# A bidirectional RWKV-7 recurrence: inverses of two steps in one batch, score matrices per head as row tiles, matmul groups kept together, and low-rank weights padded to full height

## The chip, the cores and the metric

The kernel runs on one core of one Trainium2 chip. The metric is the time of one execution on the device, in microseconds (us).

## The reference, cut to what matters

One encoder layer is applied to 1280 tokens (one request of 1024, one of 256; width 1024): a SwiGLU half step, a combined projection, two mixers (RWKV-7 in both directions, and attention), two branch projections with gates, an output projection, and a second SwiGLU half step. What is changed lies in the RWKV mixer, with 8 heads of 64 channels and two directions. Its core is a scan over the tokens for each head and direction:

```python
def _rwkv7_step(S, inp):
    r, w, k, v, kk, b = inp
    sa = jnp.einsum('dbhij,dbhj->dbhi', S, -kk)
    S = S * w[..., None, :] + sa[..., :, None] * b[..., None, :] + v[..., :, None] * k[..., None, :]
    y = jnp.einsum('dbhij,dbhj->dbhi', S, r)
    return S, y
```

The decay `w` and the rate `a` come from low-rank products: `w0 + tanh(wd) @ w_up` and `a0 + ad @ a_up`, with 64 low-rank columns for each direction.

## The kernel before

The layer runs in stages: the first SwiGLU, the projections of attention, attention interleaved with dense columns, the RWKV columns with their preparation (`columns`, `prep`), the recurrence (`run`), the branch projections, the output projection, and the second SwiGLU. A framework (Tile) gives out buffers and semaphores and orders each engine's instructions by readiness and priority; a call traced under `high_priority` goes ahead of others that are ready.

**Preparation.** `prep` works on 20 pieces: 4 pairs of heads (q) times 5 chunks of 256 tokens. For each piece and each direction d it makes two products, for the decay and for the rate: a matmul L576 with the high part of the weights (128 rows, in which the low-rank activations' high and low part lie one above the other) and a matmul L577 with the low part of the weights, which has only the 64 rows of its direction. ScalarE takes the sum through a tanh (L578). The pieces are interleaved with the projections (L165), which have no part in the change.

**Recurrence.** The scan is done in chunks of 64 tokens. A step is one chunk forward and one chunk backward for a pair of heads; there are 4 pairs of heads with 20 steps each, 80 steps in all. A step has three parts.

- `front`: the scores G of both directions, one 128x128 by 128x256 matmul for each direction (L676; the moving operand AR holds both heads side by side, with zeros in the other head's rows), masked on VectorE into `gs` (L683); two transposes of BK (L681), copied to `BKt` by ScalarE (L685); the blocks `Bm` and `Bl` cut out of `gs` by GpSimd (L692, L696).
- `inv`: the inverse of a triangular matrix for each of two heads, by doubling in fp16: a start on GpSimd and VectorE (L709, L711), five rounds of matmuls (L715), a masked eviction on VectorE (L717), matmuls (L720, L721) and an eviction on ScalarE (L723), then a correction (L726 to L733). Up to four inverses run at a time, each in its own PSUM bank.
- `chain`: what hangs on the state S. Matmuls L752 (64x64 tiles) and L756 (128x64 tiles) sum to z, ScalarE copies it (L759), L763 (64x64) makes u, ScalarE copies that (L764, L765), L771 (128x64) makes the update of S, and VectorE and GpSimd make the new S (L785, L786). L778 and L780 (128x64) make the output yp, which L792 or L794 puts into YT.

An f32 matmul is two instructions on TensorE, an fp16 one is one. `run` steps through these generators in a fixed order of ticks: in each, up to four inverses advance by one part, two places take a part of chain or front, and two take a part of `finish`, which normalizes a done pair of heads. `front` runs ahead of `chain` by up to `NB` = 7 steps.

PSUM has 8 banks: 4 for inverses, 1 for G, 1 for z, u and the update of S, 1 shared by the transposes, yp and `finish`, and 1 (`psD`) that belongs already to the next stage, so that the first products of the branch projection (L1156) can run while the recurrence still does.

Of the kernel before, what the change touches and what calls it, by code (L numbers as in the profile page):

```python
# [21 lines left out]
TT = 10  # L22
# [320 lines left out]
class Bufs:  # L343
# [5 lines left out]
    def tile(self, shape, dt, name, tag=None):  # L349
# [7 lines left out]
PQ = (4, 3)  # L357
PBT = "pb"
# [6 lines left out]
       "TT": 7, "tt": 9, "y1": 6, "zs": 2, "Sn": 3, "SP": 2}  # L365
RPB = {"i": 4, "g": 1, "z": 1, "s": 1}
# [5 lines left out]
BD = 1  # L372
# [8 lines left out]
class Rwkv:  # L381

    NB, PK, LAG, NAR, AHEAD, NI = 7, 1, 2, 8, 1, 4
# [41 lines left out]
    def prep_weights(self, q, W):  # L425
# [17 lines left out]
    def loop_consts(self, ep, cp):  # L443
# [10 lines left out]
        for i in range(self.NB):  # L454
            bm = cp.tile([128, 2, 128], F16, name=f"Bm{i}")
            bl = cp.tile([128, 2, 128], F16, name=f"Bl{i}")
# [103 lines left out]
    def prep(self, q, got, ci, W, ps):  # L560
# [10 lines left out]
        for d in range(2):  # L571
            ds_ = slice(64 * d, 64 * d + 64)
# [11 lines left out]
        o = W.tile([128, n], F32, name="go", tag="go")  # L584
# [80 lines left out]
    def front(self, pp, sd, cf, cb, W, ps, TG, res):  # L665
# [7 lines left out]
        g = ps.tile([128, 4, 128], F32, name="g", tag=TG["g"])  # L673
        for d in range(2):
            AR, BK = sd[d]
            nc.tensor.matmul(g[:, 2 * d:2 * d + 2], lhsT=BK[:, cs[d] % 4], rhs=AR[:, cs[d] % 4], start=True, stop=True)  # L676
            if d == 0:
                yield
        tr = ps.tile([128, 2, 128], F32, name="tr", tag=TG["x"])
        for d in range(2):  # L680
            nc.tensor.transpose(tr[:, d], sd[d][1][:, cs[d] % 4], self.k.ident)  # L681
        gs = W.tile([128, 4, 128], F32, name="gs", tag="gs")
        nc.vector.tensor_tensor(out=gs, in0=g, in1=self.gm, op=ALU.mult)  # L683
        BKt = W.tile([128, 2, 128], F32, name="BKt", tag="BKt")
        nc.scalar.copy(BKt, tr)  # L685
        Bm, Bl = self.Bm[self.step_no % self.NB], self.Bl[self.step_no % self.NB]
# [10 lines left out]
        TT_ = W.tile([128, 2, 128], F32, name="TT", tag="TT")  # L697
        res.update(gs=gs, BKt=BKt, UV=UV, TT=TT_, Bm=Bm, Bl=Bl)
        yield

    def inv(self, ind, W, ps, TG):

        nc = self.nc
        Bm, Bl = ind["Bm"], ind["Bl"]
        p = ps.tile([128, 4, 128], F32, name="inv", tag=TG["i"])
        m, dbl = p[:, 0:2], p.rearrange("p (h a) t -> p h a t", h=2)
        mask = lambda l: self.lv[:, l:l + 1].to_broadcast([128, 2, 128])
        tt = W.tile([128, 2, 2, 128], F16, name="tt", tag="tt")
# [4 lines left out]
        for l in range(1, 6):  # L713
            for h in range(2):
                nc.tensor.matmul(m[:, h], lhsT=Bm[:, h], rhs=tt[:, h, 0], start=True, stop=True)  # L715
            y1 = W.tile([128, 2, 128], F16, name="y1", tag="y1")
            nc.vector.tensor_tensor(out=y1, in0=m, in1=mask(l), op=ALU.mult)  # L717
            yield
            for h in range(2):
                nc.tensor.matmul(dbl[:, h, 0], lhsT=tt[:, h, 1], rhs=y1[:, h], start=True, stop=True)  # L720
                nc.tensor.matmul(dbl[:, h, 1], lhsT=y1[:, h], rhs=tt[:, h, 1], start=True, stop=True)  # L721
            tt = W.tile([128, 2, 2, 128], F16, name="tt", tag="tt")
            nc.scalar.copy(tt, dbl)  # L723
            yield
        for h in range(2):
            nc.tensor.matmul(m[:, h], lhsT=Bm[:, h], rhs=tt[:, h, 0], start=True, stop=False)  # L726
            nc.tensor.matmul(m[:, h], lhsT=Bl[:, h], rhs=tt[:, h, 0], start=False, stop=True)
        ws = W.tile([128, 2, 128], F16, name="ws", tag="y1")
        nc.vector.tensor_tensor(out=ws, in0=m, in1=tt[:, :, 0], op=ALU.subtract)
        yield  # L730
        for h in range(2):
            nc.tensor.matmul(m[:, h], lhsT=ws[:, h], rhs=tt[:, h, 1], start=True, stop=True)
        nc.vector.scalar_tensor_tensor(out=ind["TT"], in0=tt[:, :, 1], scalar=2.0, in1=m, op0=ALU.mult, op1=ALU.add)  # L733
        yield

    def chain(self, pp, sd, st, cf, cb, ind, W, ps, TG, first, early):
# [11 lines left out]
        for h in range(2):  # L748
            hs = slice(64 * h, 64 * h + 64)
            for d in range(2):  # L750
                vr = rows(1 - d)
# [560 lines left out]
```

## Time and profile before

| | |
|---|---|
| time, median of 3 runs | 3557.76 us (3557.45 to 3557.83) |
| the profiled execution: its time, its span | 3558.98 us, 3557.2 us |
| TensorE, VectorE, ScalarE, GpSimd busy | 97%, 48%, 36%, 11% of the span |
| granted TensorE clock, mean over the span | 0.988 of 2.4 GHz |

The span is the time from the first to the last instruction; the profiled execution's time is 1.8 us longer. A busy TensorE is not one at its peak: matmuls are pipelined, and the record of one is longer than the distance to the next. What a matmul takes from the others is the distance from its start to the next start, and that is how the rows of the timeline below are to be read.

### The profile page before, as it was taken

To read this page: it belongs to the slowest core of one execution; us is meant where nothing else is said; L and a number is where in the kernel's file an instruction comes from. 1 tells how busy PE (TensorE), PEld (TensorE's weight loads), DVE (VectorE), ACT (ScalarE), POOL (GpSimd) and SP (SyncE) were. 2 spreads that over 40 slices of the span, in tenths; PEclk is the share of its full clock that TensorE was granted. 3 is DMA by queue.
4 is the path that set the end of the run, shared out by engine and by line. 5 is a ranking of instruction groups with operands and counts; after the bars stand their busy time and mean duration, and the time that the engine had idled before them with its cause. 6 is when DMAs were issued, how large, how long until landed. Compare 5 with 4: busy or idle time off the path is not lost. (4 is left out here: it accounts for less than half of the span.)

```text
span 3557.2 us, 56074 instructions
## 1 busy us (share of the span) xinstructions
PE 3467.9 (97%) x22608; PEld 2907.8 (82%) x22608; DVE 1720.8 (48%) x3300; ACT 1291.6 (36%) x2524; POOL 376.7 (11%) x706
## 2 busy tenths in 40 slices
PE   8999999999899999999989999998999999999997
PEld 7888888888788888887768888888878888888886
DVE  3233333333726776648777667647332333333335
ACT  4211111111523666746556666623432111111112
POOL 0000000000301000003144444410000000000002
PEclk9999999999999999999999999999999999999999
DMA  3111111111324121224352212147221111111103
GB/s 127 42 36 36 36 48 36 42 36 35 131 83 135 59 73 45 84 77 154 130 184 85 70 54 76 41 146 236 102 83 36 42 36 36 36 45 39 36 30 119
DMA packets 155108, 264.93 MB, mean 74 GB/s; under 512 B 16864, under 2 KB 98016, under 8 KB 154720
## 3 DMA queue, kind: packets, MB, share of 16 engines
q1 hardware_dynamic: 154848, 261.34, 22.9%
q8 instruction: 178, 2.92, 0.3%
q14 instruction: 82, 0.67, 0.1%
HBM read 183.94 MB, written 74.06 MB: 73 GB/s over the span
## 5 line engine op out<-in xcount | busy, mean ns | idle before, releaser
L165 PE MATMUL pp<-hT,whi 128*128 128x512 f32 (+1 forms) x6000 | 1643.1, 360 | 7.8 <-ACT qk L950 4.9
L165 PEld LDWEIGHTS pp<-hT,whi 128*128 128x128 f32 x6000 | 1068.0, 190 | 175.6 <-ACT qk L950 5.7
L165 PE MATMUL pp<-hT,wlo 128*128 128x512 f32 (+1 forms) x3000 | 1074.4, 358 | 0.0
L165 PEld LDWEIGHTS pp<-hT,wlo 128*128 128x128 f32 x3000 | 569.3, 190 | 79.8
L141 DVE TENSOR_TENSOR wlo<-wraw,whi 128x1024 fp32r<-128x1024 f32 x125 | 154.1, 1233 | 566.7 <-ACT whi L140 566.6
L211 DVE TENSOR_TENSOR acc<-acc,pd 128x512 f32<-128x512 f32 x400 | 271.3, 685 | 203.4 <-PE pd L206 203.2
L206 PE MATMUL pd<-dh,ah 128*128 128x512 f32 x880 | 346.4, 394 | 13.8 <-DVE acc L211 13.8
L206 PE MATMUL pd<-dh,al 128*128 128x512 f32 x880 | 345.6, 393 | 0.0
L206 PE MATMUL pd<-dl,ah 128*128 128x512 f32 x880 | 345.4, 392 | 0.0
L293 POOL TENSOR_TENSOR yg<-acc,gb 128x1024 f32<-128x1024 f32 x19 | 48.2, 2544 | 2075.1 <-DMA xb<-x_d 1128.6
L723 ACT CAST tt<-inv 128x512 f16<-128x512 f32 x400 | 226.6, 588 | 90.7 <-PE inv L721 66.4
L187 DVE TENSOR_TENSOR sg<-sg,pp 128x512 f32<-128x512 f32 x132 | 79.0, 598 | 347.8 <-PE pp L165 347.8
L140 ACT CAST dh<-draw 128x1024 fp32r<-128x1024 f32 x44 | 46.0, 1046 | 528.8 <-DMA draw<-wd 528.8
L140 ACT CAST ah<-sg 128x512 fp32r<-128x512 f32 x132 | 72.2, 547 | 439.5 <-DVE sg L187 439.5
L206 PEld LDWEIGHTS pd<-dh,ah 128*128 128x128 f32 x880 | 166.7, 189 | 52.0 <-DVE acc L211 18.1
L717 DVE TENSOR_TENSOR y<-inv,lv 128x256 f16<-128x256 f32 x400 | 161.6, 418 | 83.6 <-PE inv L715 61.4
L140 ACT CAST whi<-wraw 128x1024 fp32r<-128x1024 f32 x125 | 131.1, 1049 | 194.1 <-PE pp L165 191.7
L206 PEld LDWEIGHTS pd<-dh,al 128*128 128x128 f32 x880 | 166.7, 189 | 35.3
L206 PEld LDWEIGHTS pd<-dl,ah 128*128 128x128 f32 x880 | 166.6, 189 | 33.8
L178 ACT ACTIVATE sg<-pp 128x512 f32<-128x512 f32 x132 | 69.1, 524 | 327.1 <-PE pp L165 325.8
L1156 PE MATMUL pbr<-yT,whi 128*128 128x256 f32 x640 | 124.1, 291 | 19.2 <-ACT yT L140 8.9
L720 PE MATMUL inv<-y,tt 128*128 128x128 f16 x800 | 130.7, 221 | 0.0
(228 smaller groups left out, 4868.3 us busy)
## 6 DMA issues: line engine op xcount, KB each, us to landing
wraw<-wgu SPq DMA_DIRECT2D x88, 512.0 KB, 3.5
draw<-wd SPq DMA_DIRECT2D x44, 512.0 KB, 3.8
gate_d<-go SPq DMA_DIRECT2D x16, 640.0 KB, 3.2
ar_d<-ar SPq DMA_DIRECT2D x40, 256.0 KB, 2.1
bk_d<-bk SPq DMA_DIRECT2D x40, 256.0 KB, 2.1
AR<-ar_d SPq DMA_DIRECT2D x80, 128.0 KB, 2.9
BK<-bk_d SPq DMA_DIRECT2D x40, 256.0 KB, 2.9
g<-gate_d SPq DMA_DIRECT2D x80, 128.0 KB, 3.3
```

The source lines that it names most:

```text
L140: self.nc.scalar.copy(dst_h, src)
L141: self.nc.vector.tensor_tensor(out=dst_l, in0=src, in1=dst_h.bitcast(F32), op=ALU.subtract)
L165: nc.tensor.matmul(p[:, :n], lhsT=a[:, ks], rhs=h[:, b, k], start=i == 0, stop=i == 23)
L178: nc.scalar.activation(out=sg[:, c0:c0 + n], in_=p[:, :n], func=AF.Silu)
L187: nc.vector.tensor_tensor(out=sg[:, s], in0=sg[:, s], in1=p[:, :n], op=ALU.mult)
L206: nc.tensor.matmul(p, lhsT=a[:, ts], rhs=b[:, hs], start=i == 0, stop=i == m - 1)
L211: nc.vector.tensor_tensor(out=acc[:, t, hs], in0=acc[:, t, hs], in1=p, op=ALU.add)
L293: (nc.vector if late else nc.gpsimd).tensor_tensor(out=yg, in0=y, in1=gbc, op=ALU.mult)
L717: nc.vector.tensor_tensor(out=y1, in0=m, in1=mask(l), op=ALU.mult)
L720: nc.tensor.matmul(dbl[:, h, 0], lhsT=tt[:, h, 1], rhs=y1[:, h], start=True, stop=True)
L723: nc.scalar.copy(tt, dbl)
L1156: nc.tensor.matmul(p, lhsT=a[:, ks], rhs=ys[ci][:, b, kk], start=i == 0, stop=i == 11)
```

## The change

It does five things.

- `inv` takes the four matrices of two steps at once: every tile and every instruction of it is twice as wide, the PSUM tile has two banks, and two of them are open at a time, not four. Two steps share one `Bm`, `Bl` and `TT` tile, and an inverse starts when both steps' fronts are there.
- G is made per head: four matmuls with 64 rows (heads in rows 0 to 63 and 64 to 127), 128 columns of weights and a moving operand of 128 columns, so 8 instructions of 64x128 tiles in place of 4 of 128x128. The heads go to two banks, and the transposes go into the first of these.
- `together` chains the matmuls of a group on TensorE, each behind the one before, and gives them priority. G, z, u, and the update of S with yp are such groups. In z the part with S now goes first, and the part with UV after it. The update takes the backward direction first.
- `chain` gives up control three times in a step and no more five, `front` still twice.
- In `prep` the low part of the weights has 128 rows, the other direction's set to zero by GpSimd, so L577 becomes a 128x128 matmul over all rows. The tile `go` takes its buffer from the three of `w1`.

PSUM is then 4 banks for inverses, 2 for G and the transposes, 1 for z, u and the update, 1 for yp and `finish`; `psD` is gone, and the branch projection takes all its banks when the recurrence is done.

```diff
-RWB = {... "TT": 7, "tt": 9, "y1": 6, ...}
-RPB = {"i": 4, "g": 1, "z": 1, "s": 1}
+CP = 300
+RWB = {... "TT": 4, "tt": 5, "y1": 4, ...}
+RPB = {"i": 2, "g": 1, "z": 1, "s": 1}
...
-    NB, PK, LAG, NAR, AHEAD, NI = 7, 1, 2, 8, 1, 4
+    NB, PK, LAG, NAR, AHEAD, NI = 7, 3, 2, 8, 1, 2
...
-        lo = W.tile([128, 2, 128], F32R, name="llo")
+        lo = W.tile([128, 2, 2, 128], F32R, name="llo")
         for d in range(2):
-            rs = slice(64 * d, 64 * d + 64)
-            nc.vector.tensor_tensor(out=lo[rs], in0=raw[rs, d], in1=hi.bitcast(F32)[rs, d], op=ALU.subtract)
+            rs, ot = slice(64 * d, 64 * d + 64), slice(64 - 64 * d, 128 - 64 * d)
+            nc.vector.tensor_tensor(out=lo[rs, d], in0=raw[rs, d], in1=hi.bitcast(F32)[rs, d], op=ALU.subtract)
+            nc.gpsimd.memset(lo.bitcast(F32)[ot, d], 0.0)
...
-                nc.tensor.matmul(p[:, j], lhsT=lo[ds_, j], rhs=src[ds_, d, cs], start=False, stop=True)
+                nc.tensor.matmul(p[:, j], lhsT=lo[:, d, j], rhs=src[:, d, cs], start=False, stop=True)
...
-        o = W.tile([128, n], F32, name="go", tag="go")
+        o = W.tile([128, n], F32, name="go", tag="w1")
...
-        g = ps.tile([128, 4, 128], F32, name="g", tag=TG["g"])
-        for d in range(2):
-            AR, BK = sd[d]
-            nc.tensor.matmul(g[:, 2 * d:2 * d + 2], lhsT=BK[:, cs[d] % 4], rhs=AR[:, cs[d] % 4], start=True, stop=True)
-            if d == 0:
-                yield
-        tr = ps.tile([128, 2, 128], F32, name="tr", tag=TG["x"])
+        g = ps.tile([128, 2, 4, 128], F32, name="g", tag=TG["g"])
+        with self.together() as go:
+            for d in range(2):
+                AR, BK = sd[d]
+                for h in range(2):
+                    hs = slice(64 * h, 64 * h + 64)
+                    go(g[:, h, d], lhsT=BK[hs, cs[d] % 4], rhs=AR[hs, cs[d] % 4, h], start=True, stop=True)
+        tr = g[:, 0, 2:4]
...
+    @contextlib.contextmanager
+    def together(self):
+        tc, last = self.k.tc, []
+        def go(out, **kw):
+            with tc.issue_after(last[-1].ins) if last else contextlib.nullcontext():
+                last.append(self.nc.tensor.matmul(out, **kw))
+        with tc.high_priority(offset=CP):
+            yield go
...
-        for h in range(2):
-            hs = slice(64 * h, 64 * h + 64)
-            for d in range(2):
-                vr = rows(1 - d)
-                nc.tensor.matmul(z[rows(d), h], lhsT=gs[vr, 2 * d + h, 0:64], rhs=UV[vr, d, hs], start=h == 0, stop=first and h == 1)
-        if not first:
+        with self.together() as go:
+            if not first:
+                for h in range(2):
+                    for d in range(2):
+                        go(z[rows(d), h], lhsT=sd[d][0][:, cs[d] % 4, h, 0], rhs=S[:, d], start=h == 0, stop=False)
             for h in range(2):
+                hs = slice(64 * h, 64 * h + 64)
                 for d in range(2):
-                    nc.tensor.matmul(z[rows(d), h], lhsT=sd[d][0][:, cs[d] % 4, h, 0], rhs=S[:, d], start=False, stop=h == 1)
+                    vr = rows(1 - d)
+                    go(z[rows(d), h], lhsT=gs[vr, 2 * d + h, 0:64], rhs=UV[vr, d, hs], start=first and h == 0, stop=h == 1)
...
-        psD = early.enter_context(tc.tile_pool(name="psD", bufs=1, space=PSUM))
...
-                    for _ in branch(1, yb_d, I["wbb"], WD, lambda dt, ci: psD if dt < BD or ci == 0 else ps, emit_mb, WD):
+                    for _ in branch(1, yb_d, I["wbb"], WD, lambda dt, ci: ps, emit_mb, WD):
```

## Rows read from the trace of the kernel before

**Rows 1.** Busy time and instructions of each engine, granted clock and DMA, two stretches.

```profile
core 0: us, PE busy (x) PEld busy (x) DVE busy (x) ACT busy (x) POOL busy (x), PEclk, DMA share, GB/s
1860.00:2310.00 450.00, 446.15 (x6390) 362.54 (x6390) 314.91 (x837) 300.46 (x726) 206.83 (x430) 1.00 0.23 68
...
2044.00:2068.16 24.16, 24.11 (x362) 19.70 (x361) 16.53 (x44) 15.35 (x36) 11.18 (x24) 1.00 0.20 56
```

**Rows 2.** Waits of TensorE, 1860 to 2310 us: total, times, longest.

```profile
PE inv L715 <- DVE tt L711: 3.2, 3, 1.1
```

**Rows 3.** Timeline of TensorE: start, duration, instruction.

```profile
2045.49 0.22 PE L721 MATMUL inv<-tt,y 128*128 128x128 f16 x1
2045.64 0.45 PE L763 MATMUL zu<-zs,TT 64*64 64x64 f32 x8
2046.02 0.28 PE L715 MATMUL inv<-tt,Bm 128*128 128x128 f16 x2
...
2048.43 0.33 PE L756 MATMUL zu<-Sn,AR 128*64 128x64 f32 x2
2048.69 0.23 PE L720 MATMUL inv<-y,tt 128*128 128x128 f16 x1
...
2048.81 0.22 PE L720 MATMUL inv<-y,tt 128*128 128x128 f16 x1
2048.87 0.22 PE L721 MATMUL inv<-tt,y 128*128 128x128 f16 x1
2049.02 0.45 PE L756 MATMUL zu<-Sn,AR 128*64 128x64 f32 x6
2049.39 0.29 PE L715 MATMUL inv<-tt,Bm 128*128 128x128 f16 x2
```

**Rows 4.** The same timeline, scores G and the transposes of one direction.

```profile
2052.27 0.65 PE L676 MATMUL g<-AR,BK 128*128 128x256 f32 x2
2052.76 0.38 PE L681 MATMUL tr<-ident,BK 128*128 128x128 f32 x2
2052.97 0.39 PE L715 MATMUL inv<-tt,Bm 128*128 128x128 f16 x4
```

**Rows 5.** Groups of instructions, 2044 to 2068.16 us: busy, mean ns, idle before, releasers.

```profile
L723 ACT CAST tt<-inv 128x512 f16<-128x512 f32 x20 | 11.3, 588 | 5.0 <-PE inv L721 3.8 <-POOL Bl L696 0.7 <-DVE y L717 0.2
L717 DVE TENSOR_TENSOR y<-inv,lv 128x256 f16<-128x256 f32 x20 | 8.1, 419 | 4.6 <-PE inv L715 3.1 <-ACT tt L723 1.3 <-ACT zs L759 0.2
...
L683 DVE TENSOR_TENSOR gs<-g,gm 128x512 f32<-128x512 f32 x4 | 2.7, 685 | 1.5 <-PE g L676 1.5
```

**Rows 6.** Timeline, a lightly loaded moment early in the recurrence.

```profile
1828.77 0.27 PE L715 MATMUL inv<-tt,Bm 128*128 128x128 f16 x2 [1.00 <-DVE tt L711]
...
1829.22 0.41 DVE L717 TENSOR_TENSOR y<-inv,lv 128x256 f16<-128x256 f32 x1
```

**Rows 7.** Timeline of ScalarE and VectorE, last steps of the recurrence.

```profile
2337.02 0.27 ACT L759 COPY zs<-zu 128x128 f32<-128x128 f32 x1 [1.44 <-PE zu L756]
...
2340.65 0.27 ACT L759 COPY zs<-zu 128x128 f32<-128x128 f32 x1 [2.15 <-PE zu L756]
...
2337.40 0.42 DVE L733 SCALAR_TENSOR_TENSOR TT<-tt,inv 128x256 f32<-128x256 f16 x1 [0.71 <-PE inv L732]
...
2343.02 0.29 DVE L794 TENSOR_TENSOR YT<-YT,yp 128x128 f32<-128x128 f32 x1
```

**Rows 8.** Busy time in a stretch, line L1156 alone: PE and PEld.

```profile
2310.00:2345.00 35.00, 7.86 (x39) 5.50 (x40) 1.00 0.09 28
```

**Rows 9.** Timeline of TensorE in the preparation.

```profile
1711.30 0.28 PE L576 MATMUL pl<-low,lhi 128*128 128x256 f32 x1
1711.51 0.38 PE L577 MATMUL pl<-low,llo 64*128 64x256 f32 x1
1711.82 0.73 PE L165 MATMUL pp<-hT,whi 128*128 128x512 f32 x2
...
1718.61 0.28 PE L621 MATMUL pb<-kh,bor 128*128 128x256 f32 x1
1718.72 0.39 PE L165 MATMUL pp<-hT,whi 128*128 128x512 f32 x1
```

**Rows 10.** Groups of instructions, 1577 to 1810 us.

```profile
L577 PE MATMUL pl<-low,llo 64*128 64x256 f32 x80 | 30.5, 381 | 0.0
```

**Rows 11.** Busy time, the four stretches 1577:1620, 1642:1685, 1707:1750, 1762:1810.

```profile
sum 177.00, PE 176.85 PEld 134.48 DVE 159.99 ACT 123.74 POOL 61.08; mean PE 44.21 PEld 33.62 DVE 40.00 ACT 30.94 POOL 15.27
```

More of the change, by code (lines that the diff above doesn't have):

```diff
@@ L364 @@
 RWB = {"fsq": 1, "vf": 2, "gf": 2, "BK": 8, "YT": 3, "gs": 7, "BKt": 7, "UV": 7,
-       "TT": 7, "tt": 9, "y1": 6, "zs": 2, "Sn": 3, "SP": 2}
-RPB = {"i": 4, "g": 1, "z": 1, "s": 1}
+       "TT": 4, "tt": 5, "y1": 4, "zs": 2, "Sn": 3, "SP": 2}
+RPB = {"i": 2, "g": 1, "z": 1, "s": 1}
 NGD = 5
@@ L371 @@
 D4 = 8
-BD = 1
 def dr_tiles(dr):
@@ L453, in loop_consts @@
         self.Bm, self.Bl = [], []
-        for i in range(self.NB):
-            bm = cp.tile([128, 2, 128], F16, name=f"Bm{i}")
-            bl = cp.tile([128, 2, 128], F16, name=f"Bl{i}")
+        for i in range((self.NB + 1) // 2):
+            bm = cp.tile([128, 2, 2, 128], F16, name=f"Bm{i}")
+            bl = cp.tile([128, 2, 2, 128], F16, name=f"Bl{i}")
             nc.gpsimd.memset(bm, 0.0)
@@ L696, in front @@
             nc.gpsimd.tensor_tensor(out=Bl[rs, :, rs], in0=src, in1=Bm[rs, :, rs], op=ALU.subtract)
-        TT_ = W.tile([128, 2, 128], F32, name="TT", tag="TT")
-        res.update(gs=gs, BKt=BKt, UV=UV, TT=TT_, Bm=Bm, Bl=Bl)
+        res.update(gs=gs, BKt=BKt, UV=UV, TT=self.TT2[:, j], pair=(self.Bm[i], self.Bl[i], self.TT2))
         yield
@@ L703, in inv @@
         nc = self.nc
[L704 to L708, printed above, removed]
+        Bm, Bl, TT_ = (x.rearrange("p s h t -> p (s h) t") for x in ind["pair"])
+        p = ps.tile([128, 8, 128], F32, name="inv", tag=TG["i"])
+        m, dbl = p[:, 0:4], p.rearrange("p (h a) t -> p h a t", a=2)
+        mask = lambda l: self.lv[:, l:l + 1].to_broadcast([128, 4, 128])
+        tt = W.tile([128, 4, 2, 128], F16, name="tt", tag="tt")
         nc.gpsimd.tensor_tensor(out=tt[:, :, 1], in0=Bm, in1=mask(0), op=ALU.mult)
@@ L760, in chain @@
         yield
-        for h in range(2):
-            for o in (slice(0, 64), slice(64, 128)):
-                nc.tensor.matmul(u[o, h], lhsT=TT_[o, h, o], rhs=zs[o, h], start=True, stop=True)
+        with self.together() as go:
+            for h in range(2):
+                for o in (rows(0), rows(1)):
+                    go(u[o, h], lhsT=TT_[o, h, o], rhs=zs[o, h], start=True, stop=True)
         nc.scalar.copy(UV[0:64, 0], u[0:64].rearrange("p h v -> p (h v)"))
@@ L767, in chain @@
         sp = ps.tile([128, 2, 64], F32, name="sp", tag=TG["z"])
-        for d in range(2):
-            for h in range(2):
-                hs = slice(64 * h, 64 * h + 64)
-                nc.tensor.matmul(sp[hs, d], lhsT=BKt[:, d, hs], rhs=UV[:, d, hs], start=True, stop=True)
         yp = ps.tile([128, 2, 64], F32, name="yp", tag=TG["s"])
-        for d in range(2):
-            for x in range(1 if first else 2):
-                for h in range(2):
-                    hs = slice(64 * h, 64 * h + 64)
-                    if x == 0:
-                        nc.tensor.matmul(yp[hs, d], lhsT=UV[:, d, hs], rhs=gs[:, 2 * d + h, 64:128], start=True, stop=first)
-                    else:
-                        nc.tensor.matmul(yp[hs, d], lhsT=S[:, d], rhs=sd[d][0][:, cs[d] % 4, h, 1], start=False, stop=True)
+        with self.together() as go:
+            for d in (1, 0):
+                for hs in (rows(0), rows(1)):
+                    go(sp[hs, d], lhsT=BKt[:, d, hs], rhs=UV[:, d, hs], start=True, stop=True)
+            for d in range(2):
+                for h in range(2):
+                    go(yp[rows(h), d], lhsT=UV[:, d, rows(h)], rhs=gs[:, 2 * d + h, 64:128], start=True, stop=first)
+                if not first:
+                    for h in range(2):
+                        go(yp[rows(h), d], lhsT=S[:, d], rhs=sd[d][0][:, cs[d] % 4, h, 1], start=False, stop=True)
         Sn = W.tile([128, 2, 64], F32, name="Sn", tag="Sn")
@@ L859, in run @@
             tick += 1
-            for i in range(self.NI):
+            for i in range(4):
                 while pair_n < len(pairs) and pair_n <= front_n // 4 + self.AHEAD and 2 * (pair_n - chain_n // 4) < self.NAR \
```

45 lines of the change are left out of this document (25 added, 20 removed).

## The prediction, made before the changed kernel was run

> **What bounds the kernel now.** I read the page first: TensorE is busy nearly all the time, but that says little, since the records of matmuls overlap. So I went to the two stages that the change touches. In the recurrence the stretches show TensorE busy for 446 of 450 us at the full granted clock, and every other engine below three quarters [rows 1]. The list of waits, asked for TensorE alone, is almost empty over these 450 us: 3.2 us in three waits [rows 2]. The question is then what fills TensorE, and only the timeline answers it, read from start to start. Four steps take 24.16 us (gs stands four times in that stretch) [rows 1, 5], 6.04 us a step.
>
> In that timeline an fp16 matmul of the inverse follows another by 0.06 us. When the shape of the tile changes, the next start comes 0.15 us after the last fp16 one (L721 to L763), and the way back costs more than a pitch too [rows 3]. Eight 64x64 instructions and the way back take 0.38 us, while two 128x64 instructions and the way back take 0.26 [rows 3]. Six more instructions thus cost 0.12 us, which is possible only if tiles run two at a time: a pass of 64 columns is half of a transpose's pass of 128, 0.21/2 = 0.11 us [rows 4], so some 0.05. From 0.26 = a first pass whose weights were not loaded ahead (0.11) + a last pass (0.05) + the rest, a change of shape wastes about 0.10 us. Over the 24.16 us I counted 36 such changes, 9 a step: some 0.9 of 6.04 us.
>
> **G per head.** Now: per direction two instructions, from 2052.27 to 2052.76, 0.49 us; 0.98 a step [rows 4]. After: eight instructions of 128 moving columns, 0.11 us a pass, two tiles at a time, so four places: entry 0.15 − 0.06 = 0.09; first place with its weights loaded in the open 0.21 (as 0.11 for 64 columns); two at 0.11; the last with the way back 0.11 + 0.10; 0.01 for the slower first fp16 pitch: 0.74 us. That saves 0.24. If the two row tiles do not run together, there are eight places: 0.74 + 4 × 0.11 = 1.18, a loss of 0.20. No row shows two 64x128 tiles side by side; the nearest, the 64x64 and 128x64 groups, run in pairs, and I take 0.74. So between −19 and +16 us over 80 steps.
>
> A rule speaks against this part. The Trainium skill (TensorEngine Tiling (Array Packing), section Tiling Modes, Key Properties) says that changing the mode, not just the tile, drains the engine. The trace agrees, at about 0.10 us a change, and G in row tiles adds two changes a step. The Trainium skill (TensorE: Matmul & The Clock Gate, Part 3: Packing small matmuls) says that tiles in different row groups run at once, about 4 ns apart; by that, G costs what I took. No run here shows it yet for this shape.
>
> **Groups unbroken.** A step has four groups (two shapes of z, u, and the update with yp). Of the 16 in the four steps, four are broken: three as 2 + 6, one as 4 + 4. The one shown costs 0.26 + 0.37 instead of 0.38, plus a second entry of 0.09 and 0.01: 0.35 us [rows 3]; 4 + 4 costs about 0.10 less, since the first open load is one place of two. Mean 0.32 us a step, some 26 us over 80. At worst a group still breaks: nothing is saved.
>
> **Floor of a step after:** 6.04 − 0.24 − 0.32 = 5.48, say 5.5 us of TensorE.
>
> **Inverses of two steps.** TensorE does the same 36 matmuls a step. VectorE's eviction goes from 0.419 for 256 elements to 0.685 for 512 (gs has that size), ScalarE's from 0.588 for 512 to at most 1.18 and, if its fixed part is like VectorE's (0.15), about 1.0 for 1024 [rows 5]. Per step that is less work than now, and VectorE (16.53/4 = 4.1 us a step), ScalarE (3.8) and GpSimd (2.8) [rows 1] stay below 5.5. What grows is the delay. A round now: two matmuls until VectorE starts 0.45 [rows 6], its 0.42, a hand-over taken at 0.05, four matmuls (3 × 0.06 + 0.22) with a hand-over 0.45, ScalarE's 0.59, 0.05: 2.0 us. After: 0.56 + 0.69 + 0.05 + 0.67 + 1.0 + 0.05 = 3.0. Five rounds and the correction (8 and 4 matmuls, two evictions, about 2.8) hold a PSUM pair for 17.8 us. Two pairs are open, four steps: not below 17.8/4 = 4.45 us a step even if nothing ever waits. Now it is about 12/4 = 3.0 against 6.04, half of it slack; at 5.5 the slack is 22 − 17.8 = 4.2 us, for 12 batches of matmuls and 12 evictions that each queue behind other work.
>
> The chain has less slack too. Alone it takes 3.6 us from zs to zs [rows 7]. The UV part of z used to run ahead of S; now it stands behind it, so its 0.38 us joins the loop: 4.0. In that loop three groups queue behind matmuls already begun, three copies behind ScalarE's 1.0 us evictions, and the last product on GpSimd. So I don't grant the whole 0.54 us: I take 5.8 us a step, between floor and present time, 0.24 × 80 = −19 us. Ends: 5.5 (−43) and 6.3 (+21).
>
> **The recurrence's ends, and psD.** Without `psD` the branch products that fill the last steps (39 instructions from 2310 on [rows 8], at 0.115 us some 4.5 us) come later. From the last TT to the last YT is 5.6 us now [rows 7]; after, the last inverse releases two steps, 2 × 4.0 = 8.0: +2.4. The first inverse is some 5 us later but serves two steps and the chain catches up: +2. In all +9 us, between +4 and +12.
>
> **Preparation.** L576 to L577 takes 0.21, L577 to the next 0.31 us: 0.52 [rows 9]. At full height a 256-column matmul takes 0.11 (L621), so 0.22. Saved: 0.30 × 80 [rows 10] = 24 us of TensorE. But in the four stretches in which this runs, VectorE is busy 160 of 177 us [rows 11]; TensorE would need 177 − 24 = 153, and VectorE is late next. At most 17 us can come there, the rest only if work moves between stretches. Dependent chains of a piece seldom fill an engine, so I take −10, between 0 and −24. The eight fills with zeros lie on GpSimd, idle for two thirds. `go` in the `w1` buffers waits for VectorE's scans of the piece before, and the `kd` behind it for a store to land; I cost that at nothing, because a piece has 177/20 = 9 us; without that cover the preparation gains nothing, the end 0.
>
> **Sum.** −10 − 19 + 9 = −20. The profiled execution took 3559.0 us (its span and 1.8 us around it), 1.2 above the median: 3559 − 20 − 1.2 = 3538 us.
>
> **Rivals.** (B) *The floor comes in full.* For it: TensorE has no waits now and the order holds enough ready work. Against: the slack above. 5.5 us a step: −43, preparation −17, ends +6: 3504 us. (C) *Two open inverses set the pace.* Slots, not TensorE, end each step; it decides from the point at which a pair holds its banks for 4 × 6.04 = 24.2 us, that is, when the 24 parts wait 6.4 us in all, 0.27 each. For it: the batches that they wait behind are 0.4 to 1.0 us long. Against: today the four inverses wait far more and TensorE is full all the same. At 6.3 us a step (25.2 us held): +21, preparation −6, ends +9: 3582 us. (D) *The row tiles don't pair.* The floor is 5.48 + 0.44 = 5.92, with waits about 6.1: +5, preparation −10, ends +9: 3562 us, no change to speak of.
>
> **How the numbers follow.** My forecast 0.52, with a range of its own from 3515 to 3550 us; B 0.16, C 0.17, D 0.15. Faster or slower means by over 0.2% (7 us), about what a measurement of this kernel can tell from no change. Faster: my case, B and a bit of D, 0.70; within 0.2%: most of D, 0.12; slower: C and the rest, 0.18. The range reaches to just below B and through half of the way to C and a little more: 3500 to 3570 us.
>
> **What the profile after would show.** G as one run of 8 instructions, 0.64 us from its first start to the next shape (0.74 with entry), not 1.1; no z, u or update group in two pieces; about 9 changes of shape a step still. Steps 5.8 us apart; TensorE now with waits on tt and y in its list, a few tenths of a us a step: if none, B; if ScalarE's tt and VectorE's y wait on nothing while TensorE idles over 10%, C. L577 as 128x128 with 0.11 us to the next start; VectorE above 95% in the four stretches. The prediction is wrong if the preparation doesn't shorten at all, or if the steps are spaced by the inverse and not by TensorE.

## The result and the profile after

The changed kernel takes 3729.4 us (median of 4 runs, 3725.37 to 3744.34) against 3557.66: ratio 1.0492, 95% interval 1.0471 to 1.0513. The forecast was 3538 us, its range 3500 to 3570. It was wrong in sign and by 191 us.

The place is found by three instants: the first and the last copy of z (zs) and the end of the trace.

| us | before | after | |
|---|---|---|---|
| start to the first G | 1822.4 | 1815.8 | −6.6 |
| start to the first zs | 1835.3 | 1824.1 | −11.2 |
| first to last zs, 79 steps | 505.3 | 678.8 | +173.5 |
| last yp to the end | 1214.2 | 1224.0 | +9.8 |

So all of it lies in the recurrence: 8.6 us a step in place of 6.4. The first four steps are slower by 12.1 us and the last four by 10.5; the 71 between them take 600.8 us in place of 449.9. The page already shows where to look. Its slices of TensorE (the digits are tenths of busy time) fall to 7 in the recurrence, where those of the page before stay at 8 and 9. The lines of the changed kernel come first, then the one of before:

```profile
PE 3478.3 (93%) x22928; PEld 2905.7 (78%) x22928; DVE 1708.4 (46%) x2980; ACT 1267.9 (34%) x2324; POOL 379.3 (10%) x668
...
PE   8999999999899999999777787778999999999997
...
PEclk9999999999999999999799989989999999999999
```

```profile
PE   8999999999899999999989999998999999999997
```

The stretch 1860 to 2310 us of the changed kernel, in the columns of [rows 1]:

```profile
1860.00:2310.00 450.00, 351.97 (x5050) 275.16 (x5046) 223.45 (x411) 209.32 (x410) 153.39 (x303) 0.94 0.18 53
```

TensorE was busy 446 of 450 us and is now 352; VectorE and ScalarE are under half, so no engine took its place as the bound. That is a loop of waits. The waits of TensorE in the same stretch (total, times, longest), where [rows 2] had one line of 3.2 us:

```profile
PE inv L723 <- ACT tt L731: 34.2, 75, 1.2
PE inv L728 <- DVE y L725: 20.1, 57, 0.8
PE zu L751 <- POOL Sn L806: 16.7, 23, 1.4
PE inv L740 <- DVE ws L737: 12.2, 23, 1.2
PE inv L734 <- ACT tt L731: 5.9, 11, 0.5
```

Two kinds stand here: an inverse that waits for its own eviction (L723, L728, L734, L740), and z that waits for the state (L751 behind Sn).

The timeline of ScalarE's zs shows bursts: steps 4.9 to 6.4 us apart and then a hole of 15.3 us. Such a hole comes every four steps.

```profile
2122.49 0.27 ACT L779 COPY zs<-zu 128x128 f32<-128x128 f32 x1 [0.32 <-PE zu L751]
2127.39 0.27 ACT L779 COPY zs<-zu 128x128 f32<-128x128 f32 x1 [3.03 <-PE zu L751]
2133.80 0.27 ACT L779 COPY zs<-zu 128x128 f32<-128x128 f32 x1 [2.41 <-PE zu L751]
2139.85 0.27 ACT L779 COPY zs<-zu 128x128 f32<-128x128 f32 x1 [3.11 <-PE zu L751]
2155.12 0.27 ACT L779 COPY zs<-zu 128x128 f32<-128x128 f32 x1 [0.39 <-PE zu L751]
```

VectorE's starts (L719, transpose) and ends (L741, TT) of the pairs over the same time show what the hole waits for:

```profile
2118.40 0.69 DVE L741 SCALAR_TENSOR_TENSOR TT<-tt,inv 128x512 f32<-128x512 f16 x1 [0.49 <-PE inv L740]
2125.09 0.71 DVE L719 STREAM_TRANSPOSE tt<-tt 128x512 f16<-128x512 f16 x1 [3.13 <-POOL tt L717]
2128.86 0.68 DVE L741 SCALAR_TENSOR_TENSOR TT<-tt,inv 128x512 f32<-128x512 f16 x1
2130.06 0.70 DVE L719 STREAM_TRANSPOSE tt<-tt 128x512 f16<-128x512 f16 x1
2150.97 0.69 DVE L741 SCALAR_TENSOR_TENSOR TT<-tt,inv 128x512 f32<-128x512 f16 x1 [0.49 <-PE inv L740]
```

The two slots take turns. One ends TT at 2119.09, starts again at 2125.09 and ends at 2151.66: 6.0 us empty, then 26.6 us held. 32.6 us for four steps is 8.15 a step. (The other ends at 2129.54 and starts again at 2130.06.) The empty part of the first lies on GpSimd:

```profile
2121.16 0.40 POOL L806 TENSOR_TENSOR Sn<-Sn,pc 128x128 f32<-128x128 f32 x1 [10.30 <-DVE Sn L805]
2121.84 0.98 POOL L701 TENSOR_TENSOR Bm<-gs,e 64x128 f16<-64x128 f32 x2 [0.28 <-DVE gs L688]
2122.90 0.92 POOL L705 TENSOR_TENSOR Bl<-gs,Bm 64x128 f16<-64x128 f32 x2
2123.90 1.16 POOL L717 TENSOR_TENSOR tt<-Bm,lv 128x512 f16<-128x512 f16 x1
```

GpSimd idles 10.3 us in front of the state's last product; behind it, in its order, stand the blocks of a later step and the start of the next pair. Read so, the loop is closed: inverse, chain, state, start of the next inverse, and TensorE has too little else. Whether GpSimd's order makes the hole or only takes part in it is what e4 below tries.

### The profile page after: what moved, and what is told of

Its sections match the earlier page's. It is cut to its first block, busy times and chain, and to the rows that moved or that the text cites. A ratio compares the mean times of both kernels' runs of the same rounds, so it can differ in the third digit from the quotient of the medians.

```text
span 3730.1 us, 55744 instructions
## 1 busy us (share of the span) xinstructions
PE 3478.3 (93%) x22928; PEld 2905.7 (78%) x22928; DVE 1708.4 (46%) x2980; ACT 1267.9 (34%) x2324; POOL 379.3 (10%) x668
## 3 DMA queue, kind: packets, MB, share of 16 engines
q8 instruction: 180, 2.95, 0.3%
## 5 line engine op out<-in xcount | busy, mean ns | idle before, releaser
L206 PE MATMUL pd<-dh,ah 128*128 128x512 f32 x880 | 346.5, 394 | 12.4 <-DVE acc L211 12.4
L731 ACT CAST tt<-inv 128x1024 f16<-128x1024 f32 x200 | 199.4, 1013 | 119.2 <-PE inv L729 116.9
L725 DVE TENSOR_TENSOR y<-inv,lv 128x512 f16<-128x512 f32 x200 | 137.7, 690 | 159.9 <-PE inv L723 149.9
L206 PEld LDWEIGHTS pd<-dh,ah 128*128 128x128 f32 x880 | 166.5, 189 | 50.7 <-DVE acc L211 16.9
L728 PE MATMUL inv<-y,tt 128*128 128x128 f16 x800 | 125.1, 226 | 30.1 <-DVE y L725 30.1
L723 PE MATMUL inv<-tt,Bm 128*128 128x128 f16 x800 | 83.8, 226 | 53.7 <-ACT tt L731 50.8
```

What stands on the lines that cost most here:

```text
L206: nc.tensor.matmul(p, lhsT=a[:, ts], rhs=b[:, hs], start=i == 0, stop=i == m - 1)
```

## The experiments

Two theories at first. **A**: the long pair (its delay, two slots) makes the loss. **B**: the chain does (z's part with UV behind S, groups kept whole). All ratios are to the kernel before, run in between; 95% intervals in brackets. In the table, e4 is the changed kernel with one product moved to VectorE, and e8 is e1 with the two parts of z exchanged. The cover in the last column was counted from each trace after the runs, 1880 to 2300 us: the median number of the inverses' matmuls that TensorE runs between the update sp of a step and the part of the next z that needs the new S. It was 17 before. The code fences below are cut to the lines that matter.

| label | inverses | priority | turns | us | ratio | first to last zs | cover |
|---|---|---|---|---|---|---|---|
| before | four single | no | 7 | 3557 | 1 | 505.3 | 17 |
| e3 | four single | no | 7 | 3550.8 | 0.9985 [0.9975, 0.9994] | 504.6 | 17 |
| e5 | four single | G | 7 | 3554.8 | 0.9991 [0.9982, 1.0001] | 500.9 | 18 |
| e18 | four single | no | 7 | 3562.4 | 1.0021 [1.0012, 1.003] | 510.2 | 21 |
| e14 | four single | no | 7 | 3554.5 | 0.9994 [0.9984, 1.0003] | 506.3 | 12 |
| e6 | four single | chain | 5 | 3566.9 | 1.0029 [1.0019, 1.004] | 523.3 | 9 |
| e16 | four single | no | 7 | 3564.8 | 1.0023 [1.0014, 1.0032] | 511.6 | 20 |
| e7 | four single | no | 5 | 3596.6 | 1.0108 [1.0091, 1.0125] | 539.6 | 8.5 |
| e10 | four single | yes | 7 | 3603.3 | 1.0134 [1.0117, 1.0151] | 551.0 | 6 |
| e1 | four single | yes | 5 | 3608.1 | 1.0146 [1.0131, 1.0161] | 552.5 | 3 |
| e8 | four single | yes | 5 | 3612.1 | 1.0162 [1.0144, 1.0181] | 559.7 | 3 |
| e17 | five single | no | 7 | 3577.1 | 1.0056 [1.0041, 1.0071] | 519.4 | 17 |
| e2 | two pairs | no | 7 | 3593.0 | 1.0103 [1.0088, 1.0118] | 542.5 | 8.5 |
| e12 | two pairs | G | 7 | 3613.9 | 1.0157 [1.0142, 1.0173] | 563.6 | 9 |
| e13 | two pairs | no | 7 | 3603.6 | 1.0133 [1.0118, 1.0148] | 543.9 | 11 |
| e15 | two pairs, staggered | no | 7 | 3633.4 | 1.0214 [1.0197, 1.0231] | 577.3 | 12 |
| e11 | two pairs | no | 5 | 3631.1 | 1.0204 [1.0189, 1.022] | 576.1 | 7 |
| e9 | two pairs | yes | 7 | 3673.4 | 1.0327 [1.0312, 1.0343] | 623.1 | 2 |
| e4 | two pairs | yes | 5 | 3699.9 | 1.0409 [1.0392, 1.0426] | 649.6 | 3 |
| after | two pairs | yes | 5 | 3729.4 | 1.0492 [1.0471, 1.0513] | 678.8 | 2 |

### The change cut in two: all but the pairs, and the pairs alone

e1 is the changed kernel with the `inv`, slots and buffers of before; e2 is the kernel before with the paired `inv` alone.

```diff
 e1   RPB = {"i": 4, ...}   NB, PK, LAG, NAR, AHEAD, NI = 7, 1, 2, 8, 1, 4
 e2   RPB = {"i": 2, ...}   NB, PK, LAG, NAR, AHEAD, NI = 7, 3, 2, 8, 1, 2
```

> The whole change except the pairing of inverses: four inverses of one step each are open again, with their old buffers. Theory A (the paired inverses set the pace, because only two are open and each takes too long from start to end): the steps are again spaced by TensorE, at 5.5 to 5.9 us instead of 8.2, and the time is 3505 to 3545 us. Theory B (the chain sets the pace, because z's part with UV now waits for S and the groups are kept whole): the steps stay near 8 us and the time stays above 3680 us.

> The kernel before with the pairing of inverses alone; G, chain, transposes, the low-rank weights and psD as before. Theory A: the steps are spaced 7.5 to 8.5 us apart and the time is 3680 to 3740 us. Theory B: steps near 6.0 us, 3550 to 3590 us.

Measured: 3608.1 and 3593.0. Neither theory stands: each half costs something, about +51 and +36 us, together half of 172. The halves make each other worse. In e1 the waits of TensorE, 1860 to 2310, are those of the state:

```profile
PE zu L748 <- POOL Sn L803: 19.8, 31, 2.1
PE inv L720 <- ACT tt L728: 6.0, 21, 0.5
PE sp L748 <- ACT UV L783: 3.2, 17, 0.3
```

In e2 they are those of the inverse:

```profile
PE inv L718 <- ACT tt L726: 10.1, 18, 1.0
PE inv L729 <- ACT tt L726: 2.0, 6, 0.3
```

### The parts of the first half alone

e3: lo at full height, and `go` in `w1`. e5: lo, and G as row tiles in its group, without `psD`. e6: lo, and the new chain with its groups (5 turns).

```diff
 e3   matmul(p[:, j], lhsT=lo[:, d, j], rhs=src[:, d, cs], ...)
 e5   e3 + go(g[:, h, d], lhsT=BK[hs, cs[d] % 4], rhs=AR[hs, cs[d] % 4, h], ...) - psD
 e6   e3 + chain() and together() of the changed kernel
```

> The kernel before with the low-rank lo weights at full height alone (and go in w1's buffers). If the prediction's term holds, 10 us come back: 3543 to 3552 us. If VectorE holds the preparation as a whole, nothing changes: 3556 to 3560 us. If all of TensorE's 24 us come back: 3534 us.

> Full-height low-rank weights, and of the recurrence G as row tiles alone (kept together, with priority, the transposes in its banks, no psD); chain and inverses as before. The prediction's terms: 0.24 us a step saved, 7 us lost at the end without psD, so 3551 - 19 + 7 = 3539 us, 3530 to 3548. If G's rows, its two banks or its priority are what costs time in the version without pairs (3608 us): above 3580 us.

> Full-height low-rank weights, and of the recurrence the new chain alone (groups kept together with priority, z's part with S ahead of its part with UV, three parts and no more five); G, transposes, psD and inverses as before. The prediction's term: 0.32 us a step saved, so 3525 us, 3518 to 3540. If the new chain is what costs time in the version without pairs: 3585 to 3620 us.

Measured: 3550.8, 3554.8, 3566.9; G and the chain missed what was expected by 16 and 42 us. Lo is worth 5 us; it is the only part that helps alone. G shortens the recurrence by 3.7 us against e3 (504.6 to 500.9), and what follows the recurrence grows by 3.3 us (1216.2 to 1219.5) without `psD`. It does more than that where the steps run evenly: the 71 steps from the fifth to the 76th zs take 439.9 us in e5 and 448.8 in e3, while the first four take 44.1 in place of 38.2. The chain costs 16. Without any interaction lo, G and chain would make 3550.8 + 4.0 + 16.1 = 3571; e1 has 3608, so 37 us come from G and chain together.

### Where z stands: the priority, the order in z, and GpSimd

e7: e1 without the priority. e8: e1 with z's UV part ahead of its S part, as before. e4: the changed kernel with the state's product on VectorE, out of GpSimd's order.

```diff
 e7  -        with tc.high_priority(offset=CP):
     -            yield go
     +        yield go
 e8   (the two loops of z exchanged)
 e4  -            nc.gpsimd.tensor_tensor(out=Sn, in0=Sn, in1=pcs, op=ALU.mult)
     +            nc.vector.tensor_tensor(out=Sn, in0=Sn, in1=pcs, op=ALU.mult)
```

> The version without pairs (3608 us), with the groups of matmuls still behind one another in order but without priority over what else is ready. Theory P (the priority puts z's group into TensorE's queue before S is there, and all that stands behind it waits): TensorE's waits on S fall from 18 to under 6 us in 400 and the time to 3530 to 3570 us. Theory U (z's part with UV behind S makes the loop longer): 3595 to 3620 us, as before the edit.

> The version without pairs (3608 us), with z's part with UV ahead of its part with S again, as two groups, each with priority. Theory U (the loop of the chain is longer by 0.38 us a step, and the chain sets the pace): 30 us come back, 3570 to 3590 us. Theory P (TensorE stands still at the head of its queue while S is not there): the part with S still stands there too early, at most 10 us come back: 3595 to 3615 us.

> The changed kernel with one instruction moved: the product that ends a chain step (S times its decay) runs on VectorE and no longer on GpSimd, where in the changed kernel it waits up to 10.4 us for the chain while the start of the next pair's inverse is queued behind it. If that queue is what makes the pairs start late (theory C), the hole of 10 us in each four steps closes and the steps come 5.8 to 6.5 us apart: 3550 to 3610 us. If the pairs are held by their own rounds and by two open places (theory A), at most 3 us in four steps come back: 3670 to 3730 us.

Measured: 3596.6, 3612.1, 3699.9. The order inside z is no cause (e8). e7 missed what its theory P said: without priority TensorE's waits for S fall only from 17.4 to 12.5 us (1880 to 2300 us), the time only by 12. That time lies where theory U had it, but e8 speaks against U, so neither of the two is the whole cause. GpSimd's order is worth about 30 of 172 us, but the holes stay, as theory A of e4 had it: a slot then stands empty for 1.7 us (median) and is held for 28.8. GpSimd's longest waits of the changed kernel and then of e4, 1860 to 2310 us, show it: the wait for the state goes, and the one for gs grows in its place.

```profile
POOL Bm L701 <- DVE gs L688: 173.6, 54, 10.9
POOL Sn L806 <- DVE Sn L805: 102.8, 30, 10.4
```

```profile
POOL Bm L701 <- DVE gs L688: 270.0, 47, 11.2
```

### Priority and turns, with and without pairs

Theory **T** as recorded: with 5 turns of the loop a step for chain and front (7 before), these are emitted in bursts, and with 7 turns the holes go. Theory P: the priority holds TensorE in front of the chain's waits. Each is undone alone and both together, on e1 and on the changed kernel. e9 and e10 put the two lost yields back; e11 takes the priority away; e13 and e16 do both.

```diff
         st["S"] = Sn
+        yield
...
             nc.vector.tensor_tensor(out=dst, in0=dst, in1=yp, op=ALU.add)
+        yield
```

> The changed kernel with the two yields put back that the chain lost: chain and front together again take 7 turns of the emission loop a step, as before, in place of 5, while an inverse still takes 14 ticks for its slot. Theory T (bursts of emission: with 5 turns a step the chain and the fronts run ahead in 10 of 14 ticks, then nothing is left for them until the next inverses, so each engine's fixed order holds four steps in a burst and then a hole of 10 to 16 us): the spacing of the zs copies becomes even, the holes over 10 us go, and the time falls by over 60 us, to 3560 to 3660. Theory R (the holes are the time that the dependent loop of pair inverse, chain and front takes, whatever the turns): within 25 us of the changed kernel, 3690 to 3750.

> All parts of the change but the paired inverses (3608 us as it ran), with the same two yields put back in the chain. Theory T: the steps come evenly, the priority's stalls shrink, 3540 to 3575. Theory R (the order in turns does not matter, the high priority of the chain's matmuls makes TensorE wait for the state): 3595 to 3615.

> The changed kernel without the high priority of the groups in together (the groups stay unbroken). Without pairs this gave back 12 us of 57. Theory T (turns): 10 to 30 us less than the changed kernel, 3695 to 3720, and the holes of about 15 us per four steps stay. Theory P (the priority holds TensorE in front of the chain's waits while the inverses behind it could run, and with pairs a wait costs twice): 3580 to 3650.

> The changed kernel without the high priority and with the two yields of the chain put back (each alone gave back 98 and 56 us of 172). If the two causes are separate, what stays is the paired inverses' own cost: 3580 to 3610. If both are one cause (the order in which the chain comes between the inverses), the second adds nothing: 3622 to 3640. Slot theory (4 steps take what one slot of a pair holds its banks from its transpose to the end of TT, plus the time until the slot's next transpose; 24.8 + 2.1 us in pairs alone, 30.8 + 5.9 less overlaps in the changed kernel): hold 25 to 26.5 us, and the sum of both is four steps.

> Lo, G as row tiles, the chain's new order of matmuls and no psD, single inverses, without high priority and with the old 7 turns. The same with both (all but pairs) took 3608 us, without priority 3597, with 7 turns 3603. If priority and turns are the whole of what G and the chain cost together, 3545 to 3565. If G and the chain cost something of their own together (G's group and the chain's groups cut up the same stretches of TensorE, 11 to 12 shape changes a step in place of 9), 3570 to 3592.

Times in us, all with lo, G as row tiles, the chain's new order, and without `psD`:

| | no priority, 7 turns | 5 turns | priority | both |
|---|---|---|---|---|
| four single | 3564.8 | 3596.6 | 3603.3 | 3608.1 |
| two pairs | 3603.6 | 3631.1 | 3673.4 | 3729.4 |
| pairs cost | 39 | 35 | 70 | 121 |

With single inverses either of the two costs 32 to 39 us, and both no more than 43: undoing one alone gains little (e10 only 5 us, which theory T had not expected). With pairs they cost 28 and 70, and both 126, more than the sum. e11 fell where its theory P had it. e9 fell between its two ranges with the holes still there (13 to 16 us every four steps), so the bursts of theory T are not the cause. e13 and e16, which undo both, came in the ranges for two causes that leave nothing but the pairs' own cost, e16 at the upper end.

The cover was counted only afterwards. The priority pulls z ahead, and with 5 turns fewer parts of the inverses are laid between two parts of the chain. The cover goes the same way as the times: 20, 8.5, 6, 3 in the first row, 11, 7, 2, 2 in the second. A moment of before and then one of the changed kernel show it:

```profile
2034.04 0.22 PE L771 MATMUL sp<-UV,BKt 128*64 128x64 f32 x1
...
2035.80 0.40 POOL L786 TENSOR_TENSOR Sn<-Sn,pc 128x128 f32<-128x128 f32 x1
...
2037.10 0.28 PE L756 MATMUL zu<-Sn,AR 128*64 128x64 f32 x2
```

```profile
2124.52 0.45 PE L751 MATMUL sp<-UV,BKt 128*64 128x64 f32 x8
...
2126.06 0.40 POOL L806 TENSOR_TENSOR Sn<-Sn,pc 128x128 f32<-128x128 f32 x1 [1.00 <-DVE Sn L805]
...
2126.51 0.45 PE L751 MATMUL zu<-Sn,AR 128*64 128x64 f32 x8 [0.86 <-POOL Sn L806]
```

Before, the new S is there 0.9 us ahead of z, with 17 of the inverses' matmuls since sp. In the changed kernel TensorE has run 2 of them and stands for 0.86 us, until S ends. How often z starts within 0.1 us of the end of S, from 1880 to 2300 us and of the steps in which GpSimd's product is found ahead of z (before: 2 of 52):

| | no priority, 7 turns | 5 turns | priority | both |
|---|---|---|---|---|
| four single | 6 of 48 | 10 of 49 | 40 of 46 | 41 of 46 |
| two pairs | 9 of 49 | 10 of 47 | 37 of 42 | 32 of 37 |

So the priority puts z so close behind sp that S ends last, and pairs raise the price. The 5 turns alone take cover away too, but S seldom ends last; how they cost 32 and 28 us is not shown by this count. Nor is the cover the whole account: e14 has 12 and a recurrence of 506.3 us, next to 504.6 in e3, while e15 has one more than e13 and is slower by 30 us. In e16 the waits of TensorE are gone, and the stretch reads as [rows 1] does:

```profile
PE zu L748 <- POOL Sn L802: 0.9, 6, 0.2
PE inv L725 <- DVE y L722: 0.7, 3, 0.2
```

```profile
1860.00:2310.00 450.00, 447.84 (x6622) 356.50 (x6622) 312.92 (x830) 296.34 (x720) 207.90 (x430) 1.00 0.21 63
```

### What stays: the pairs, the phase, and the groups without priority

e12: lo, G and pairs with the old chain. e15: e13 with the two slots' starts 7 ticks of 14 apart. e17: e3 with five single slots, the bank from `psD`. e14: e3 and the chain's groups without priority, 7 turns. e18: e5 without its priority.

```diff
 e15  if slots[j] is None and len(packs) > 1 and packs[1][1] + self.LAG <= tick and tick % 14 == 7 * j:
 e17  RPB = {"i": 5, ...}   RWB = {... "tt": 11, "y1": 7, ...}   NB, PK, LAG, NAR, AHEAD, NI = 7, 1, 2, 8, 1, 5
```

> The change without its chain: paired inverses, lo at full height, scores G as row tiles without psD, and the chain with its old matmul order and its old 7 turns. The parts added up: pairs +35, lo -7, G +4, so 3585 to 3600 if pairs and G do not interact. Theory T says the interaction of +80 sits in the shortened chain, so this run stays at 3580 to 3605. Theory R (row tiles of G hold two banks with one buffer, and the pairs want them in bursts): over 3640.

> As the run with no priority and seven turns, and the two slots of pairs may start only 7 ticks of 14 apart (in the runs so far the two TT end 6 to 10 us apart and then 18 to 21 us pass, so both pairs' 1.0 us evictions queue behind each other). Phase theory: hold falls towards 22 us, steps even, 10 to 40 us less than the run without it. Rival (the phase is made by the engines' waits, not by the loop, or a later start costs what the queueing did): within 8 us of it or slower.

> The kernel before with lo at full height (3551 us), single inverses, but five slots in place of four, the fifth bank taken from psD (which costs about 6 to 9 us after the recurrence). Slot theory in its strong form (four slots set the pace before the change too: 21.8 + 2.7 us for four steps against 25.4 measured): the steps shorten towards TensorE's floor of about 5.9 us, 25 to 35 us, so 3520 to 3540. Rival (TensorE was the bound before, its queue stretched the hold): the recurrence stays within 5 us, 3552 to 3562.

> Lo at full height and the chain's unbroken groups in the new order of matmuls, without high priority and with the old 7 turns; single inverses, old G, psD kept. With priority and 5 turns this part alone cost 16 us over lo. Order theory (priority and turns made the whole cost of the chain's part; unbroken groups save up to 0.32 us a step on TensorE): 3530 to 3550. Slot theory (a slot is held 21.8 us and opens again after 2.7 us whatever TensorE's floor is, so what TensorE saves in drains comes back as a wait): 3546 to 3556, the same as lo alone.

> Lo and G as row tiles with the old chain, without the high priority of G's group (3555 us with it). Candidate for the fastest version. If G's priority pulls the group ahead of ready inverses, 3540 to 3550. If G's group without it is cut up by other matmuls and pays more shape changes (as the chain's groups were: 9.2 changes a step against 7.9), 3552 to 3565.

Measured: 3613.9, 3633.4, 3577.1, 3554.5, 3562.4. e12 lies between its theories: G as row tiles, with its priority and its banks, costs beside pairs 24 us more than the parts added up (3593.0 − 6.6 + 4.0 = 3590), so the chain does not hold the whole interaction. Staggering made it slower by 30 us: a slot is held no shorter (25.1 us) and stands empty longer, so this way of parting the two starts is no help. A fifth slot made the kernel slower too, by more than either of its theories had it, and TensorE then waits 19.1 us for the starts of inverses:

```profile
PE inv L716 <- DVE tt L712: 19.1, 23, 1.0
```

The time of a slot, medians from 1880 to 2300 us: from its transpose to the end of its TT, and from there to its next transpose. With four steps open their sum is about the time of four steps. In the changed kernel the two slots differ, so both are given.

| | held | empty | four steps, mean |
|---|---|---|---|
| before | 21.8 | 2.7 | 25.4 |
| e16 | 22.4 | 2.7 | 25.4 |
| e2, pairs | 24.8 | 2.1 | 27.4 |
| e13, pairs | 24.3 | 2.7 | 26.7 |
| after, pairs | 26.9 and 32.6 | 6.0 and 0.5 | 33.7 |

That sum must come out as four steps wherever slots are refilled at once, before the change too, where TensorE was full; so it does not show by itself that slots are the bound. e17 speaks against it for before: with five slots each stands empty for 11.1 us, and nothing is won. It does not settle it, since `front` still runs ahead by no more than 7 steps and the starts come late. For the pairs, TensorE's idle time (in e13 19 of 450 us) with waits for ScalarE's tt shows that a slot's delay, not TensorE, ends some steps.

e14 and e18 say what the groups are worth. Without priority the matmuls keep their order, but others come between them: changes of the tile's shape, counted from the traces, are 9.2 a step in e14, 12.2 in e18 and 12.4 in e16, against 8.9 before, and no time is saved. With priority the groups hold (7.9 in e6, 8.2 in e1, 8.1 in the changed kernel).

No version beats e3, lo alone, at 3550.8 us.

## Why the prediction was wrong

**Preparation: right, size a little off.** Forecast −10 us; the first G comes 6.6 us earlier, and lo alone gave 5 to 7. The full-height matmul and the one ahead of it can take about what was forecast (here 0.12 + 0.12 from start to start, where [rows 9] gave 0.21 + 0.31):

```profile
1709.01 0.28 PE L577 MATMUL pl<-low,lhi 128*128 128x256 f32 x1
1709.13 0.28 PE L578 MATMUL pl<-low,llo 128*128 128x256 f32 x1
1709.25 0.40 PE L165 MATMUL pp<-hT,wlo 128*128 128x512 f32 x1
```

Over all pieces the medians are 0.18 + 0.12, so the pair saves 0.22 us and not 0.30. VectorE was named as late next, above 95%; it is busy 162 of 177 us (92%), TensorE 161. So neither is full. TensorE's idle time there lies in front of L577, L622 and L623, which wait for ScalarE's sao and for kh: chains inside a piece.

**G per head: the group's time right, the gain half.** Forecast 0.64 us from the first start to the next shape; in a timeline of the changed kernel, to be set beside [rows 4], it is 2089.06 to 2089.70. D falls. Of the 0.24 us a step that this was to save, e5 shows 0.13 in its even part (439.9 against 448.8 us in 71 steps), and the first steps took most of that back; where the other half went is not shown.

```profile
2088.68 0.45 PE L751 MATMUL zu<-zs,TT 64*64 64x64 f32 x8
2089.06 0.71 PE L751 MATMUL g<-AR,BK 64*128 64x128 f32 x8
2089.70 0.34 PE L282 MATMUL pr<-ident,fsq 128*128 128x128 f32 x1
```

The Trainium skill (TensorE: Matmul & The Clock Gate, Part 3: Packing small matmuls) says that tiles in different row groups run at once. The trace agrees: eight instructions in 0.64 us, where eight one after another were worked out as 1.08 (0.64 + 4 × 0.11).

**Groups unbroken: right in shape but for G, and not free.** From 1880 to 2300 us no group of z or u is cut; of 50 updates 6 are cut between sp and yp, and of 49 groups of G 20 are in two pieces. 8.1 changes of shape a step were found (about 9 forecast), and in e6 the matmuls of z and u take 1.12 us a step from start to next start, 1.34 before. But the saving came at a price that the prediction set at nothing. It never names the priority that keeps a group whole, and never asked whose place the group takes.

**Ends and psD: one part right, the others short.** The forecast +9 was 4.5 for the branch products without `psD`, 2.4 for the last two steps and 2 for the start. The last two came as forecast: 8.0 us from the last TT to the last YT, 5.5 before. What follows the last yp, the part for `psD`, grew by 9.8 us in the changed kernel and by 5.3 in e5. From the first G to the fifth zs it takes 58.3 us in place of 50.7.

**The step before.** The sum goes by 6.04 us a step, read from four steps. Over the even part of before it is 449.9 / 71 = 6.34, so the four were fast ones. The sum uses differences and hardly changes; C's point of 24.2 us would be 25.4.

**The step that failed** is "So I don't grant the whole 0.54 us: I take 5.8 us a step". It allows 0.3 us of waits a step on a floor of 5.5. In the changed kernel TensorE idles 98 of 450 us, and the step is 8.6: with pairs, priority and turns cost 126 us, where nothing was put down for them. The list of what would queue was there (three groups, three copies, the product on GpSimd), but two edits had no line in the sum: the priority, and the five turns for seven. They shape the order in which every engine gets its work, and the prediction took that order as given. The trace of before had the number: 17 of the inverses' matmuls (median), 2.87 us from sp to the next z on average, stand where the update goes through VectorE and GpSimd. After the change 2 stand there, and TensorE waits for Sn (16.7 us) and, with pairs, far longer for the inverses' own evictions (34.2 + 20.1 + 12.2 + 5.9 us).

The Trainium skill (PSUM — Partial Sum Buffer, Engine vs sequencer instructions) says that the other engines' queues are strictly first in, first out and that matmuls start in program order. The traces fit that: with 2 matmuls of cover in place of 17, TensorE stands 23 times for Sn in front of z, and GpSimd stands 10.3 us in front of a state's product. That work behind them was ready by then was not read from the traces.

**The rivals.** C's mechanism is the nearest: from 24.2 us of held banks on, two pairs were to set the pace, 3582 us. Pairs alone hold 24.8 us and gave 3593. But C's price, 25.2 us held, was that of the pair on its own; beside priority and turns the means are 30.1 held and 3.5 empty. It got 0.17, against which stood that "the four inverses wait far more and TensorE is full all the same": true of four inverses, not of two pairs (e13 idles 19 of 450 us with nothing else changed against e16, which idles 2).

**The sum as measured.** Lo, G and the chain's order without priority, with 7 turns and without `psD`: +7 (e16 against 3557.7). Pairs: +39. Priority and turns: +43 with single inverses. What these last cost more beside pairs than beside single inverses: +83 (126 − 43). Together 172, the measured 171.7. This split is by the runs; which wait of the changed kernel each of the 83 us belongs to is only argued from the timeline.

**Open.** Why G beside pairs costs 24 us more than its parts, and why staggering cost 30, was not tried further. A smaller offset of the priority was not tried, nor fronts that run further ahead than 7 steps, which two pairs or five slots may want. No run changes the cover alone.

## What to carry to other kernels

A priority or a shorter turn does not only move the work that it names: in engines that keep their order it takes cover away from every dependent step behind it. Before giving a dependent chain priority, count in the trace how much other work stands between a step's last product and its first use (here 17 matmuls, 2.9 us), and whether the step's result is there when its use comes up; if the use starts as soon as the result ends, the engine that was full has begun to wait. Here 12 matmuls of cover lost next to nothing with single inverses (e14), and 9 lost 16 us (e6). Batching independent work makes fewer, longer items in flight, so it should be tried with the order unchanged, and each part of such a change alone and then in twos, since here 83 of 172 us lay between the parts.

## What the runs showed of the hardware

Over 1860 to 2310 us the granted clock is 1.00 before and 0.94 in the changed kernel. The total of TensorE's holes does not tell it: e6 and e17 idle 23 and 24 of the 450 us and have 1.00, e7 idles 17 and has 0.95, e9 idles 85 and has 0.98. In the one fall looked at closely, TensorE had been busy for only 2.95 of 5 us shortly before; then whole slices stand at about 0.50, the lower of its two levels (1.2 of 2.4 GHz):

```profile
2010.00:2015.00 5.00, 2.95 (x46) 2.25 (x46) 2.72 (x4) 2.34 (x4) 0.00 (x0) 1.00 0.00 0
2015.00:2020.00 5.00, 5.00 (x74) 4.39 (x70) 2.02 (x6) 2.28 (x6) 2.86 (x5) 1.00 0.05 13
2020.00:2025.00 5.00, 4.74 (x57) 3.70 (x58) 4.32 (x16) 1.64 (x6) 1.54 (x2) 0.54 0.06 16
2025.00:2030.00 5.00, 4.52 (x51) 3.65 (x49) 3.10 (x6) 2.10 (x6) 1.94 (x5) 0.50 0.00 0
```

So busy time flatters such slices: 51 to 57 matmuls in 5 us that count as almost busy, against 74 (their mix of shapes differs). Where this happens, the kernel can pay twice, in the wait and in the slower work after it. By an estimate from these rows it is at most 0.06 × 450 = 27 us of the stretch in the changed kernel, and 0.05 × 450 = 22 us in e7, which would be much of the 32 us that e7 loses against e16. How much of the 172 us that is was not separated.
